# Hybrid conformer / RG-LRU decoder layer on eight cores: earlier first weights, a reordered gate schedule in two slots, and a last norm in place

## The chip, the cores and the metric

The kernel runs on all eight cores of one Trainium2 chip. Each core computes its own 1152 token rows (1024 of the prompt, 128 of the samples), and reads 1024 earlier prompt rows for the convolutions and the recurrent state. The cores exchange no data while they run. The metric is the device time of the slowest core, in microseconds (us).

Some executions of this program fall in a slower state, in which one die (cores 0 to 3, or 4 to 7) shows a lower granted TensorE clock. Times are set side by side only when they were taken on the same chip; across chips, ratios to the kernel before are compared.

Engine names are those of the profile: PE is TensorE, DVE is VectorE, ACT is ScalarE, POOL is GpSimd, SP is SyncE. POOL and SP mainly issue DMA transfers here.

## The reference

One layer: a mixer with two head groups on one shared input projection, then a gated MLP with a short convolution. Both are wrapped in RMS norms.

```python
def mixer(xn, ...):
    a_val, a_gate, b_x, b_gate = split(xn @ w_in)
    u  = a_val * sigmoid(a_gate)                     # group A, 8 x 128 channels
    ca = silu(layer_norm(causal_dwconv(u, 31 taps)))
    xc = causal_dwconv(b_x, 4 taps)                  # group B, 8 heads x 128 channels
    h  = rglru(xc, wa, wx, ...)                      # two gates per head, then a scan over tokens
    cb = h * gelu(b_gate)
    return concat(ca, cb) @ w_out

def layer(x):
    x = x + rms_norm(mixer(rms_norm(x, g_mix_pre)), g_mix_post)
    f = (gelu(g) * v) @ w_down       # g, v = halves of causal_dwconv(rms_norm(x) @ w_up, 3 taps)
    return x + rms_norm(f, g_ffn_post)
```

The width is 2048, the MLP's inner width 6144. Inputs and outputs are float32; matmul operands are bf16.

## The kernel before

The kernel is a list of operations with keys for what they read and write. A small scheduler derives the waits from the keys, and each engine runs its operations in the order written. Three places matter.

**The start.** Token tiles x0, x1, ... (128 rows of 2048 floats, 1 MB each) come on the SP queue. ACT and DVE norm a tile, PE transposes it, and ACT and DVE copy it out of PSUM (`p0_turn`). The first projection ("groups" g0 to g4 of columns) needs the transposed tiles and four weight tiles `wu0` to `wu3` (1 MB read, 512 KB stored each), which come on the POOL queue.

```python
p0_load(0)
load("sp", r_su, vecs[:, 0:V_FW], ...)
load_w(4, after=[("xt0",)])          # the four weight loads wait until x0 has landed
for n in range(1, 5):
    p0_load(n)
# ...
def next_tile(n):
    p0_turn(n)        # transpose tile n and copy it out of PSUM
    p0_norm(n + 2)    # norm tile n+2; this also issues a later reload of its buffer
next_tile(0)
next_tile(1)
for g in range(5):
    early(g, lambda j: next_tile(2 * g + 2 + j))     # projection of group g
    if g < 2:
        conv_diag(g)                                 # one DVE multiply of 4.28 us
```

**The slots.** In slots j = 3 to 7 PE alternates between the projections of group A and the two gates of a group B head. ACT and DVE work on what PE has left in PSUM.

```python
if j in (3, 4):
    P_gate(j - 3 + (j == 4), "wab"); P_sig(...)   # first gate: head 0 in slot 3, head 2 in slot 4
    if j == 3:
        P_conv(1)
# ... (v projection, head 0's or 2's second gate and scan)
if j == 3:
    P_gate(1, "wab"); P_sig(1, "p1", V_BA)
    bc = conv(j, [0])
    P_gate(1, "wxb"); P_sig(1, "p3", V_BX)
    conv_out(j, bc)
    P_in(1); P_mult(1)
    P_bx(2); P_evac(2)
    P_scan(1)
    P_conv(2)
```

**The tail.** The down-projection runs twice over halves of the inner width. The first half leaves partial sums in device memory (`f_scr`). The second half adds them, norms, adds the residual h (from `h_scr`) and stores y. There are nine token tiles t and four column groups fg.

```python
def hh_load(t):       # residual h of tile t, 1 MB, into one of three buffers, SP queue
    load("sp", r_x, T[f"hh{t % 3}"][:], h_scr[...], ..., [(f"hh{t % 3}", 0), (f"hh{t % 3}", 1)])
def down_load(i):     # 256 KB of partial sums into one of three prv buffers, SP queue
    load("sp", r_ld, T["prv"][:, i % 3, :], f_scr[rows, 512 * fg:512 * fg + 512], ...)
# ... for each item (fg, t):
    tt(f, out, T["prv"][:, i % 3, :], ALU.add, ...)            # "the add": frees the PSUM bank
    act(T["dj"][:], f, AF.Square, ..., accum=sc[:, fg:fg + 1])
    tt(f, f, T["grow3"][:, cs], ALU.mult, ...)
    # ... for fg == 3: sum, Ln, Exp, then
    stt(hh[:, 0:1536], f3, r, hh[:, 0:1536], ALU.mult, ALU.add, ...)
    stt(hh[:, 1536:2048], f, r, hh[:, 1536:2048], ALU.mult, ALU.add, ...)
    load("sp", r_out, y_d[rows, 0:1536], hh[:, 0:1536], ...)   # y stores, out of hh
    load("sp", r_out, y_d[rows, 1536:2048], hh[:, 1536:2048], ...)
    if t < 6:
        hh_load(t + 3)                                         # must wait for those stores
```

All buffers lie at fixed addresses in a table `AT`.

## Time and profile before

| What | Before |
|---|---|
| time, median of 3 runs | 1873.48 us (1871.01 to 1875.07) |
| spans of the eight cores in the profile | 1861.7 to 1869.5 us |
| PE busy, slowest core | 94% of the span |
| g0 / g2 start (median of cores) | 24.9 / 54.9 us |
| slot 2's convolution starts (mean of cores) | 136.7 us |
| from there to slot 4's convolution (mean) | 102.7 us |
| last matmul ends (mean) | 1833.2 us |
| tail: last matmul to the end (mean) | 32.5 us |

The last five rows are read from each core's timeline. They cut the kernel into four stages.

From the page of the profile (slowest core, core 4): busy time, share and number of instructions of each engine, then the shares of the chain of work that ended last.

```profile
PE 1751.6 (94%) x10302; PEld 916.9 (49%) x10470; DVE 988.8 (53%) x997; ACT 569.0 (30%) x1016; POOL 128.5 (7%) x239
PE 84%; DMA 7%; DVE 3%; ACT 3%; issue 2%; SPq 0%; POOL 0%; DVEq 0%; ACTq 0%; POOLq 0%
```

PE is the limit almost everywhere. What the change can win are the stretches in which PE waits, and the tail after its last matmul.

Start, timeline of PE before, core 4 (start, duration, engine, line, operation, output<-inputs, and in brackets the idle time before it and what ended it):

```profile
24.78 1.23 PE L379 MATMUL ps<-sb_xna_137,sb_wu_192 128*128 128x160 bf16 x8 [3.87 <-DVE sb_xna_137 L352]
...
29.51 1.47 PE L474 MATMUL ps<-sb_identb,sb_xs_107 128*128 128x128 bf16 x16
...
56.58 1.87 PE L379 MATMUL ps<-sb_xna_137,sb_wu_192 128*128 128x256 bf16 x8 [1.33 <-DVE sb_xna_137 L352]
```

These are the start of g0, the transposes of tile x2, and the start of g2. Both groups wait for a DVE copy of a transposed tile (`sb_xna`).

Start, timelines of ACT, then of DVE, before, core 4:

```profile
13.19 1.91 ACT L348 ACTIVATE sb_xs_102<-sb_xt_101 128x2048 bf16<-128x2048 f32 x1 [1.38 <-DMA sb_xt_101<-xall]
...
18.99 1.91 ACT L348 ACTIVATE sb_xs_107<-sb_xt_106 128x2048 bf16<-128x2048 f32 x1 [1.71 <-DMA sb_xt_106<-xall]
```

```profile
21.68 2.35 DVE L373 SCALAR_TENSOR_TENSOR sb_xs_107<-sb_xt_106,sb_tiny,sb_grow_51 128x2048 bf16<-128x2048 f32 x1 [2.78 <-ACT sb_tiny L346]
23.95 0.68 DVE L352 COPY sb_xna_137<-ps 128x1024 bf16<-128x1024 bf16 x1
```

ACT begins x1 at 13.19 and x2 at 18.99, each the moment the tile lands. The DVE lines show an order: the copy of tile x1 out of PSUM, which g0 needs, stands behind the norm of tile x2. So g0 waits for x2 to land although it does not use it.

Start, chain of work that ended last, before (start, duration, what):

```profile
10.84 24.98 DMA sb_wu_195<-w_in
36.57 10.33 DMA sb_xt_101<-xall
```

The last of the four weights takes from 10.84 to 35.82; only then is x0's buffer reloaded, because the weight load was given x0's buffer as a thing it reads.

Slots, waits of PE between 180 and 260 us, before, core 4 (waiting instruction, what ended the wait: us in all, times, longest):

```profile
PE ps L379 <- DVE sb_xcpbY L352: 4.2, 1, 4.2
PE ps L379 <- ACT sb_p3Y L346: 2.7, 2, 1.3
PE ps L379 <- ACT sb_p_68 L346: 1.3, 1, 1.3
...
```

Tail, chain before, core 4:

```profile
1836.56 9.18 DMA y<-sb_hh_108
...
1846.33 7.27 DMA sb_prv<-f_scr
...
1854.04 0.70 DVE sb_fl L364
```

A y store holds its `hh` buffer; the reload of that buffer waits for it on the SP queue; the load of the next partial sums stands behind that reload. The last matmul ended at 1834.6 on this core, but the last add could only start at 1854.04, when its partial sums had landed.

The last stores, timeline of the SP queue before, core 4 (span 1869.5):

```profile
1859.06 0.99 SPq L382 DMA_DIRECT2D y<-sb_hh_108  x2
```

The issue of the last two stores ends at 1860.05. The program ends 9.5 us later.

### The profile page before, as it was taken

To read this page: it belongs to the slowest core of one execution; us is meant where nothing else is said; L and a number is where in the kernel's file an instruction comes from. 1 tells how busy PE (TensorE), PEld (TensorE's weight loads), DVE (VectorE), ACT (ScalarE), POOL (GpSimd) and SP (SyncE) were. 2 spreads that over 40 slices of the span, in tenths; PEclk is the share of its full clock that TensorE was granted. 3 is DMA by queue.
4 is the path that set the end of the run, shared out by engine and by line. 5 is a ranking of instruction groups with operands and counts; after the bars stand their busy time and mean duration, and the time that the engine had idled before them with its cause. 6 is when DMAs were issued, how large, how long until landed. Compare 5 with 4: busy or idle time off the path is not lost.

```text
span 1869.5 us, 33611 instructions; the slowest of 8 cores (1861.7 to 1869.5 us)
## 1 busy us (share of the span) xinstructions
PE 1751.6 (94%) x10302; PEld 916.9 (49%) x10470; DVE 988.8 (53%) x997; ACT 569.0 (30%) x1016; POOL 128.5 (7%) x239
## 2 busy tenths in 40 slices
PE   6899899989987999999999999999999999999992
PEld 4675455644432444555555544444555555544441
DVE  3654455458875565666666630003666666652244
ACT  4552442368882443222222211111222222211111
POOL 0010000001120001000000000001000000000000
PEclk9899999999997999999999999999999999999996
DMA  8572243223278439543444326557343344455766
GB/s 218 175 160 41 41 83 53 37 35 58 36 123 214 158 143 195 103 68 68 68 68 68 68 61 119 119 118 128 67 69 67 67 70 68 69 137 119 186 187 201
DMA packets 54262, 193.22 MB, mean 103 GB/s; under 512 B 7233, under 2 KB 11201, under 8 KB 46785
## 3 DMA queue, kind: packets, MB, share of 16 engines
q0 software_dynamic: 29232, 106.41, 34.6%
q1 hardware_dynamic: 24850, 84.65, 13.7%
q8 instruction: 84, 1.38, 0.3%
q14 instruction: 96, 0.79, 0.1%
HBM read 266.52 MB, written 32.35 MB: 160 GB/s over the span
## 4 chain that ended last, share of the span: by engine, by line
PE 84%; DMA 7%; DVE 3%; ACT 3%; issue 2%; SPq 0%; POOL 0%; DVEq 0%; ACTq 0%; POOLq 0%
PE ps L379 83%; DMA sb_wo_213<-w_out 1%; DMA sb_wu_195<-w_in 1%; DMA sb_prv<-f_scr 1%; DMA y<-sb_hh_108 1%; PE ps L474 1%; DMA sb_xt_101<-xall 1%; ACT L346 1%; DMA y<-sb_hh_104 0%; PE ps L1139 0%; DMA sb_xt_96<-xall 0%; DVE sb_fl L364 0%; DMA y<-sb_hh_99 0%; DVE sb_ht L373 0%; DVE sb_xc_126 L373 0%
## 5 line engine op out<-in xcount | busy, mean ns | idle before, releaser
L352 DVE COPY sb_ve_120<-ps 128x1026 f32<-128x1026 f32 (+1 forms) x48 | 36.4, 801 | 297.8 <-PE ps L379 297.8
L352 DVE COPY sb_ve_134<-ps 128x1026 f32<-128x1026 f32 (+1 forms) x48 | 36.4, 800 | 113.9 <-PE ps L379 113.9
L373 DVE SCALAR_TENSOR_TENSOR sb_ov_136<-sb_ve_134,sb_vecs,sb_ov_136 128x1184 f32<-128x1184 f32 x48 | 69.7, 1451 | 5.3 <-DVE sb_ov_136 L373 0.5
L373 DVE SCALAR_TENSOR_TENSOR sb_og_135<-sb_ge_133,sb_vecs,sb_og_135 128x1184 f32<-128x1184 f32 x48 | 69.7, 1451 | 5.0
L373 DVE SCALAR_TENSOR_TENSOR sb_ov_122<-sb_ve_120,sb_vecs,sb_ov_122 128x1184 f32<-128x1184 f32 x48 | 69.7, 1451 | 5.0
L373 DVE SCALAR_TENSOR_TENSOR sb_og_121<-sb_ge_119,sb_vecs,sb_og_121 128x1184 f32<-128x1184 f32 x48 | 69.7, 1451 | 5.0
L344 ACT COPY sb_dstg<-ps 128x512 f32<-128x512 f32 x36 | 20.9, 586 | 159.6 <-PE ps L379 159.6
L379 PE MATMUL ps<-sb_ubf_110,sb_diag_109 128*128 128x342 bf16 (+3 forms) x527 | 62.3, 279 | 0.7 <-ACT sb_ca_199 L346 0.7
L379 PE MATMUL ps<-sb_ubf_124,sb_diag_123 128*128 128x342 bf16 (+3 forms) x527 | 62.3, 279 | 0.0
L344 ACT COPY sb_ffo<-sb_ve_134 128x32 f32<-128x32 f32 x24 | 5.3, 220 | 183.1 <-DVE sb_ve_134 L352 183.1
L344 ACT COPY sb_ffo<-sb_ve_120 128x32 f32<-128x32 f32 x24 | 5.3, 219 | 175.4 <-DVE sb_ve_120 L352 175.4
L346 ACT ACT_TABLE_LOAD x38 | 48.8, 1283 | 26.4 <-PE ps L379 14.1
L346 ACT ACTIVATE sb_og_135<-sb_og_135 128x1184 f32<-128x1184 f32 x24 | 28.6, 1190 | 82.5 <-DVE sb_og_135 L373 82.5
L379 PEld LDWEIGHTS ps<-sb_ubf_110,sb_diag_109 128*128 128x128 bf16 x527 | 44.8, 97 | 17.5 <-issue 0.9
L379 PEld LDWEIGHTS ps<-sb_ubf_124,sb_diag_123 128*128 128x128 bf16 x527 | 45.0, 97 | 17.1
L346 ACT ACTIVATE sb_og_121<-sb_og_121 128x1184 f32<-128x1184 f32 x24 | 28.6, 1190 | 79.6 <-DVE sb_og_121 L373 79.6
L344 ACT COPY sb_ge_119<-ps 128x1026 f32<-128x1026 f32 (+1 forms) x48 | 31.3, 704 | 34.2 <-PE ps L379 34.2
L344 ACT COPY sb_ge_133<-ps 128x1026 f32<-128x1026 f32 (+1 forms) x48 | 31.4, 706 | 27.4 <-PE ps L379 27.4
L379 PE MATMUL ps<-sb_xna_137,sb_wu_192 128*128 128x512 bf16 (+2 forms) x157 | 31.1, 348 | 8.0 <-DVE sb_xna_137 L352 5.2
L379 PE MATMUL ps<-sb_xn_139,sb_wp_216 128*128 128x512 bf16 (+1 forms) x188 | 34.8, 324 | 0.7 <-ACT sb_ge_119 L344 0.6
L379 PE MATMUL ps<-sb_xn_139,sb_wp_225 128*128 128x512 bf16 (+1 forms) x188 | 34.9, 324 | 0.2
L379 PE MATMUL ps<-sb_xn_142,sb_wp_217 128*128 128x512 bf16 (+1 forms) x190 | 35.0, 324 | 0.1
(728 smaller groups left out, 4053.4 us busy)
## 6 DMA issues: line engine op xcount, KB each, us to landing
f_scr<-sb_dstg SPq DMA_DIRECT2D x36, 256.0 KB, 3.1
sb_prv<-f_scr SPq DMA_DIRECT2D x36, 256.0 KB, 6.4
sb_xt_96<-xall SPq DMA_DIRECT2D x5, 1024.0 KB, 7.3
sb_x_0_117<-xall SPq DMA_DIRECT2D x5, 1024.0 KB, 4.8
h_scr<-sb_x_0_117 SPq DMA_DIRECT2D x5, 1024.0 KB, 3.9
sb_xt_101<-xall SPq DMA_DIRECT2D x4, 1024.0 KB, 10.3
sb_xt_106<-xall SPq DMA_DIRECT2D x4, 1024.0 KB, 13.9
sb_wp_214<-w_up POOLq DMA_DIRECT2D x8, 512.0 KB, 6.0
```

What stands on the lines that cost most here:

```text
L344: S.op("act", lambda e: e.copy(out=out, in_=in_), reads, writes)
L346: S.op("act", lambda e: e.activation(out=out, in_=in_, func=func, scale=scale, bias=bias), reads, writes)
L352: S.op("dve", lambda e: e.tensor_copy(out, in_), reads, writes)
L373: S.op("dve", lambda e: e.scalar_tensor_tensor(out, a, s, b, op0, op1), reads, writes)
L379: S.op("pe", lambda e: e.matmul(out, lhsT, rhs, start=start, stop=stop, skip_group_check=skip), reads, writes)
L474: S.op("pe", lambda e, pb=pb, j=j, k=k: e.transpose(pb[:, 128 * j:128 * j + 128], xs[:, 128 * k:128 * k + 128], identb[:]), [ks, "identb"] ...
```

## The change

The intent is to close the three gaps. (1) The four first weight tiles are issued at once, tiles x2 to x4 each wait for one of them, and x0's buffer is no longer tied to the weights. (2) In slots 3 and 4 head 1's and head 2's gates get more projection work between them. (3) The partial sums are loaded straight into their final buffers, the norm is done in place, and the residuals of tiles 6 to 8 go early into buffers that are free by then. The address table changes as a whole.

```diff
 # (1) start
-        load_w(4, after=[("xt0",)])
-        for n in range(1, 5):
-            p0_load(n)
+        load_w(4)
+        p0_load(1)
+        for n in range(2, 5):
+            p0_load(n, [(f"wu{n - 1}",)])
...
             if g == 2:
-                load_w(6, after=[("xt3",)])
+                load_w(6, after=[("xt4",)])
 # (2) slots
-            if j in (3, 4):
-                P_gate(j - 3 + (j == 4), "wab")
-                P_sig(j - 3 + (j == 4), "p1", V_BA)
-                if j == 3:
-                    P_conv(1)
-            else:
+            if j == 3:
+                P_gate(0, "wab")
+                P_sig(0, "p1", V_BA)
+                P_conv(1)
+            elif j > 4:
...
-            proj(bv, "v", j, ACT3)
+            proj(bv, "v", j, ACT3, only=0)
+            proj(bv, "v", j, ACT3, only=1)
+            if j == 4:
+                P_gate(2, "wab")
+                P_sig(2, "p1", V_BA)
+            proj(bv, "v", j, ACT3, only=2)
...
             if j == 3:
+                bc = conv(j, [0])
                 P_gate(1, "wab")
                 P_sig(1, "p1", V_BA)
-                bc = conv(j, [0])
+                conv_out(j, bc)
+                bx2 = triple()
+                P_bx(2, bx2)
                 P_gate(1, "wxb")
...                                   # head 2's P_conv now ahead of head 1's P_scan
 # (3) tail
-            ("fl", [2, 512], F_, 22.9, 24),
-            ("prv", [3, 512], F_, 22.9, 24), ("dstg", [3, 512], F_, 21, 22),
+            ("fl", [3, 512], F_, 22.9, 24), ("fh", [3, 512], F_, 22.9, 24),
+            ("dstg", [3, 512], F_, 21, 22),
...
+            def f_load(t, fg):      # partial sums straight into f3 (SP queue), fg 3 into the fl ring (POOL queue)
+                f, kf = f_place(t, fg)
+                load("sp" if fg < 3 else "pool", ..., f, f_scr[...], [("f_scr", t, fg)], [kf])
+            def f_place(t, fg):
+                if fg < 3:
+                    return T[f"f3{t}"][:, fg, :], (f"f3{t}", fg)
+                return T["fl"][:, t % 3, :], ("fl", t % 3)
+            def h_place(t): ...     # tiles 0-5: hh ring; tiles 6-8: f30..f32 and fh (POOL queue)
...
-                tt(f, out, T["prv"][:, i % 3, :], ALU.add, PK(b) + [("prv", i % 3)], [kf])
+                tt(f, out, f, ALU.add, PK(b) + [kf], [kf])
...
+                for c0, c1 in ((0, 768), (768, 1536)) if tt_ == 8 else ((0, 1536),):
+                    kk = k3[c0 // 512:(c1 + 511) // 512]
+                    stt(f3[:, c0:c1], f3[:, c0:c1], r, ha[:, c0:c1], ALU.mult, ALU.add, kk + [kr] + kha, kk)
+                    load("sp", r_out, y_d[rows, c0:c1], f3[:, c0:c1], kk, [])
+                stt(f, f, r, hb, ALU.mult, ALU.add, [kf, kr, khb], [kf])
+                if tt_ < 3:
+                    hh_load(tt_ + 3)
+                load("sp", r_out, y_d[rows, 1536:2048], f, [kf], [])
                 if tt_ < 6:
-                    hh_load(tt_ + 3)
+                    f_load(tt_ + 3, 3)      # into the buffer that the store above has just been given
+                if tt_ < 3:
+                    hh_load(tt_ + 6)
```

## The prediction

> **What bounds it now.** TensorE: the page gives PE 94% busy of 1869.5 us; the chain of waits is 84% PE. The stage table (windows) shows 99% or more for most of 800 to 1830 us. Only idle PE can give time (core 4):
> - Start: PE busy 35 of the first 60 us. Chain: "DMA sb_wu_195", 25 us. The four weight loads waited on tile xt0 and so count as its readers; the slot's reload is issued only at 36.0 us, when the last weight lands (35.8). Group g2 starts at 56.6 us.
> - Slots 3 and 4 (180 to 240 us): PE waits 1.3 (p3Y), 1.3 (p), 4.2 (xcpbY), 0.2 and 1.3 us (p3Y), 8.4 together; matmuls after the 4.2 us gap run slow (2.45 for 1.67, 0.98 for 0.58 us), another 1.2.
> - Tail: last matmul ends at 1834.5, span at 1869.5: 35 us (31 to 35 over the cores). Chain: y store, h reload, prv load, in order on the SP queue: each prv load sits behind an h reload that waits 5 to 9 us for its buffer's y store.
>
> **What the change does.**
> 1. Start. Weights go out at 2 us with x0 and x1; x2 to x4 wait for weights 1 to 3; the reload of x0's slot no longer waits for weight 3. At the 3.5 us per MB read that the first 36 us show (9.4 MB in 34 us), weight 3 lands near 27 us, tile 5 near 37 (43 before). But x2 lands near 24 instead of 19, and VectorE, in order, evacuates tile 1 only after normalising tile 2: g0 starts at 29 to 31 instead of 24.8. g2 starts near 52. Gain 4.5 us (0 to 8).
> 2. Slots. Head 1's two gates get 6.7 us of projection between them; head 2's conv goes ahead of head 1's scan and its gate 15 us later, inside the v projection. One wait of about 0.4 us stays. Gain 9 us.
> 3. Tail. Partial sums are preloaded into f3 in place (no prv), results written in place, h of tiles 6 to 8 fetched early into freed f3 buffers. Behind a y store sit only fl loads: tiles 7 and 8 wait for the fl stores of 4 and 5 (stores take 5 to 9 us, loads 6). I estimate the last add 3 to 4 us after the last matmul (20 before), then 4 us to the first half store and 9 us for the last megabyte (10 before). The Trainium skill ("DMA: Bandwidth & Descriptors", Anatomy of one DMA) puts about 2 us fixed on each DMA; here a 256 KB store takes 3.1 us, which agrees, so splitting helps little. Tail 16.5 instead of 35 us: gain 18 (14 to 22).
>
> Moved buffers change nothing I can find.
>
> **Sum.** 4.5 + 9 + 18 = 31.5, perhaps 2 more for less spread between cores: about 1840 us, 8 in 10 between 1830 and 1852. Faster by over 2% needs 1836.7: chance 0.32; within 2% 0.67; slower 0.01.
>
> **Right if** g2 starts 2 to 7 us earlier; no PE wait over 1 us between 180 and 240 us; the span ends 14 to 20 us after the last matmul. **Wrong if** weights starve x1 (g0 after 33 us); ScalarE's table switches delay head 2 and its gate still waits; the fl ring delays the last add beyond 8 us; or PE loses time later.

## More of the kernel before

**The end of the program.** The SP engine waits for every DMA that was ever issued.

```python
fin = Op("sp", None, False)
fin.deps = [o for n in self.NAMES for o in self.streams[n] if o.is_dma]
```

## The result

The changed kernel took 1862.74 us, the median of 4 runs (1861.02 to 1864.39). The kernel before took 1873.48 us beside it on the same chip (median of three runs; a fourth, slow one took 2124.55). The ratio is 0.9944, with a 95% interval of 0.9925 to 0.9964: about 10.5 us faster, which is "within 2%". Executions over 1.5% slower than the fastest of the same kernel are left out of the means. All ratios here are the mean time of one kernel's runs over that of the other's of the same rounds, so they are not quite the ratio of the quoted medians. The result lies 10.7 us above the predicted range of 1830 to 1852 us.

Stage by stage, mean over the eight cores in the two profiled executions:

| Stage | Before | After | Gain | Predicted gain |
|---|---|---|---|---|
| start, up to slot 2's convolution | 136.7 | 143.1 | -6.4 | +4.5 |
| slot 2's to slot 4's convolution | 102.7 | 93.6 | +9.1 | +9 |
| from there to the last matmul | 1593.9 | 1594.0 | -0.1 | 0 |
| tail | 32.5 | 26.6 | +5.9 | +18 |
| mean span | 1865.7 | 1857.2 | +8.5 | |

The four gains add up to the change of the mean span. One stage came out as predicted, one gained a third of what was expected, and one lost. Of the 31.5 us predicted, 23 are missing: 10.9 at the start and 12.1 in the tail.

The page after (slowest core, core 1), the same two lines:

```profile
PE 1761.6 (95%) x10470; PEld 916.4 (49%) x10470; DVE 989.3 (53%) x998; ACT 569.3 (31%) x1016; POOL 134.5 (7%) x254
PE 89%; DMA 4%; ACT 2%; DVE 2%; issue 2%; POOL 0%; DVEq 0%; ACTq 0%; POOLq 0%; SPq 0%
```

PE's busy time seems to have grown by 10 us. It has not: the trace before lacks 168 matmul records (10302 against 10470).

Start, timeline of PE after, core 1:

```profile
25.08 1.86 PE L474 MATMUL ps<-sb_identb,sb_xs_102 128*128 128x128 bf16 x16 [9.68 <-DVE sb_xna_137 L352]
34.75 1.23 PE L379 MATMUL ps<-sb_xna_137,sb_wu_192 128*128 128x160 bf16 x8 [7.81 <-DVE sb_xna_137 L352]
...
38.71 1.06 PE L474 MATMUL ps<-sb_identb,sb_xs_107 128*128 128x128 bf16 x16
...
61.45 1.07 PE L379 MATMUL ps<-sb_xna_137,sb_wu_192 128*128 128x256 bf16 x8 [3.16 <-DVE sb_xna_137 L352]
```

The first line is the transposes of x1. g0 starts 10.0 us later than on core 4 before, the transposes of x2 9.2 us later, g2 4.9 us later. (As medians over the cores these are 10.5, 10.3 and 7.2 us; core 4 before had the latest g2 of all.) Once g0 runs it no longer waits for a weight, but it runs late.

Start, timelines of ACT, then of DVE, after, core 1:

```profile
19.23 1.91 ACT L348 ACTIVATE sb_xs_102<-sb_xt_101 128x2048 bf16<-128x2048 f32 x1 [9.20 <-DMA sb_xt_101<-xall]
...
28.96 1.91 ACT L348 ACTIVATE sb_xs_107<-sb_xt_106 128x2048 bf16<-128x2048 f32 x1 [6.18 <-DMA sb_xt_106<-xall]
```

```profile
31.66 2.35 DVE L373 SCALAR_TENSOR_TENSOR sb_xs_107<-sb_xt_106,sb_tiny,sb_grow_51 128x2048 bf16<-128x2048 f32 x1 [6.72 <-ACT sb_tiny L346]
33.92 0.68 DVE L352 COPY sb_xna_137<-ps 128x1024 bf16<-128x1024 bf16 x1
```

This is the cause at the start. x1 lands at 19.2 instead of 13.2, x2 at 29.0 instead of 19.0. The copy that g0 waits for is still the next DVE instruction after the norm of x2.

Where the bandwidth went is in the list of DMA issues after, core 1, 0 to 40 us (transfer, queue, KB, us from issue to landing):

```profile
sb_wu_192<-w_in POOLq DMA_DIRECT2D x1, 512.0 KB, 9.9
sb_wu_193<-w_in POOLq DMA_DIRECT2D x1, 512.0 KB, 16.2
```

The first two weights were issued at 2.2 and 2.8 us, so they landed at about 12 and 19 us, before g0 could use them. x1 was issued at 2.8 us and landed at 19.1 (13.1 before). The Trainium skill ("DMA: Bandwidth & Descriptors", Queues, rings and completion order) says that each DMA engine takes turns between the queue rows it has work for, a packet at a time. This trace agrees, counted in the packets that the profile lists. DMA queues after, core 1, first from 9 to 12 us, then from 12 to 16 us (q0 carries the weights, q1 the tokens; number of packets, MB written, share of the 16 DMA engines):

```profile
q0 software_dynamic: 109, 0.38, 87.5%
q1 hardware_dynamic: 114, 0.09, 16.0%
```

```profile
q1 hardware_dynamic: 79, 0.64, 51.6%
q0 software_dynamic: 79, 0.32, 50.7%
```

From 12 to 16 us x1's packets (8 KB each) and the weights' (4 KB written, from 8 KB of floats) alternate one for one, so x1 gets half of the DMA time. From 9 to 12 us the token queue got as many turns as the weights, but almost no bytes: 88 of its 114 packets are the 32-byte packets of `flags`, a small table of 4 KB that stands ahead of x1 on the SP queue. On this core `flags` landed at 12.6 us, against 9.9 on core 4 before; over all cores it was 12.5 to 14.4 against 8.6 to 10.9. So part of x1's delay was spent on 4 KB of small packets, each of which waited for its turn beside a 4 KB packet of weights. No run moves `flags` behind x1, so what that would gain is not shown.

Slots, waits of PE between 180 and 260 us, after, core 1:

```profile
PE ps L379 <- DVE sb_ubf_124 L364: 1.2, 1, 1.2
PE ps L379 <- ACT sb_p1Y L346: 0.2, 1, 0.2
```

8.4 us of waits have become 1.4. (The lines of other engines are left out here and above. The prediction had allowed no wait over 1 us in slots 3 and 4; one of 1.2 us is there.) The 4.2 us wait before had a second cost: the matmuls after it took 2.45 us for groups that take 1.67 elsewhere. The Trainium skill ("TensorE: Matmul & The Clock Gate", Part 1) has TensorE fall to half its clock after an idle window of about 3.4 us. This trace agrees: the granted clock was 0.50 from 222.1 to 223.2 us, just after the 4.2 us wait (before, core 4), and in the timeline of PE above, the 16 transposes after a 9.68 us wait took 1.86 us, those without a wait 1.06. The start is not so sharp: before, on core 4, the transposes of x1 took 1.87 us after a wait of only 2.93.

Tail, chain after, core 1:

```profile
1805.82 16.11 DMA y<-sb_fl
...
1825.00 7.24 DMA sb_fl<-f_scr
1832.33 0.70 DVE sb_fl L364
...
1847.93 2.39 DMA y<-sb_f_191
```

The old chain of `hh` and `prv` is gone. A shorter one of the same kind took its place: a 256 KB store of y out of an `fl` buffer took 16.11 us, and the load of tile 6's partial sums into the same buffer had to wait for it. (The store landed at 1821.9 and the load was issued at 1825.0. This further 3.1 us is there on every core, where the other loads of the ring mostly follow within 0.6 us; the trace does not show what it is.) The add of tile 6 starts at 1832.33, after the last matmul (1831.0). Tiles 7 and 8 follow at the pace of DVE and ACT, 5.5 to 5.8 us each.

Tail, timeline of DVE after, core 1: the add of tile 6, the add of tile 8, and the second half of tile 8's result.

```profile
1832.33 0.69 DVE L364 TENSOR_TENSOR sb_fl<-ps,sb_fl 128x512 f32<-128x512 f32 x1 [7.81 <-DMA sb_fl<-f_scr]
...
1843.66 0.68 DVE L364 TENSOR_TENSOR sb_fl<-ps,sb_fl 128x512 f32<-128x512 f32 x1
...
1850.41 1.02 DVE L373 SCALAR_TENSOR_TENSOR sb_f_191<-sb_f_191,sb_ssf,sb_f_185 128x768 f32<-128x768 f32 x1 [2.61 <-DMA y<-sb_f_191]
```

The last line is a wait that the change made itself. Keys are kept per 512 columns. The halves (0, 768) and (768, 1536) both hold the key of columns 512 to 1023, so the second half waits for the first half's store to land.

The last store, timeline of the SP queue after, core 1 (span 1862.8):

```profile
1852.22 0.33 SPq L382 DMA_DIRECT2D y<-sb_fl  x1
```

This store has 256 KB, and the one just ahead of it 384 KB, against 1 MB before. Yet the program ends 10.3 us after this issue. That raises the question whether the 9.5 us before were the time of the last megabyte at all. One difference between the compiled programs points elsewhere: SP's final list has 178 wait instructions before and 194 after. And the traces record when a store lands: on core 4 before, the last one landed 3.5 us after the start of its issue, 6.3 us before the end; on core 1 after, 2.7 us after, 7.9 us before the end.

### The profile page after: what moved, and what is told of

The parts are those of the page before. It is cut to its first block, busy times and chain, and to the rows that moved or that the text cites. A ratio compares the mean times of both kernels' runs of the same rounds, so it can differ in the third digit from the quotient of the medians.

```text
span 1862.8 us, 33795 instructions; the slowest of 8 cores (1849.1 to 1862.8 us)
## 1 busy us (share of the span) xinstructions
PE 1761.6 (95%) x10470; PEld 916.4 (49%) x10470; DVE 989.3 (53%) x998; ACT 569.3 (31%) x1016; POOL 134.5 (7%) x254
## 4 chain that ended last, share of the span: by engine, by line
PE 89%; DMA 4%; ACT 2%; DVE 2%; issue 2%; POOL 0%; DVEq 0%; ACTq 0%; POOLq 0%; SPq 0%
PE ps L379 88%; DMA sb_wo_213<-w_out 1%; DMA sb_wu_194<-w_in 1%; DMA y<-sb_fl 1%; PE ps L474 1%; DMA sb_xt_98<-xall 1%; PE ps L1146 0%; DMA sb_fl<-f_scr 0%; ACT L346 0%; DVE sb_fl L364 0%; DVE sb_ht L373 0%; ACT sb_xs_1_132 L348 0%; ACT sb_t_1_128 L346 0%; ACT sb_dj L348 0%; DVE sb_t_1_129 L729 0%
## 5 line engine op out<-in xcount | busy, mean ns | idle before, releaser
L346 ACT ACT_TABLE_LOAD x38 | 48.8, 1283 | 28.8 <-PE ps L379 16.5
L379 PE MATMUL ps<-sb_xna_137,sb_wu_192 128*128 128x512 bf16 (+2 forms) x160 | 29.7, 333 | 17.1 <-DVE sb_xna_137 L352 14.9
L344 ACT COPY sb_ge_133<-ps 128x1026 f32<-128x1026 f32 (+1 forms) x48 | 31.4, 707 | 27.4 <-PE ps L379 27.4
L379 PE MATMUL ps<-sb_xn_139,sb_wp_214 128*128 128x512 bf16 (+1 forms) x192 | 35.2, 325 | 0.5 <-DVE sb_xn_139 L352 0.5
```

Of the source, the lines that this page charges most:

```text
L344: S.op("act", lambda e: e.copy(out=out, in_=in_), reads, writes)
L346: S.op("act", lambda e: e.activation(out=out, in_=in_, func=func, scale=scale, bias=bias), reads, writes)
L379: S.op("pe", lambda e: e.matmul(out, lhsT, rhs, start=start, stop=stop, skip_group_check=skip), reads, writes)
```

## The experiments

All fourteen kernels gave correct results. Each was timed in five rounds beside the kernel before on its own chip. "Worth" figures are differences of ratios, times 1872 us. With the intervals of the table such a figure is uncertain by about 3 us either way, and with the first run's 0.9944 as the base instead of 0.9954 all would shift by 1.9 us; the stage times are the firmer evidence. The mean start of slot 2's convolution ("start stage") and the tail are read as in the tables above.

The main theory was this: at the start the weights take the bandwidth that x1 and x2 need; the slots work as planned; and the tail loses its gain to the `fl` ring and to something fixed at the end. The rivals: the new address table costs time everywhere; the start's loss comes from the added waits on x2 to x4; the end is really the time of the last stores.

| Kernel | Time (us), median | Ratio to before | 95% interval |
|---|---|---|---|
| a: start undone | 1856.57 | 0.9911 | 0.9898 to 0.9924 |
| b: tail undone | 1870.15 | 0.9986 | 0.9973 to 1.0000 |
| c: slots undone | 1874.27 | 1.0006 | 0.9994 to 1.0018 |
| d: no waits on x2 to x4 | 1859.88 | 0.9929 | 0.9917 to 0.9941 |
| the change, again | 1863.54 | 0.9954 | 0.9942 to 0.9967 |
| e: fl ring in weight buffers | 1865.06 | 0.9978 | 0.9948 to 1.0009 |
| f: fewer last waits | 1854.04 | 0.9905 | 0.9891 to 0.9918 |
| g: copies first | 1858.59 | 0.9947 | 0.9917 to 0.9977 |
| h: a, f and a new tail | 1847.43 (1837.93 undisturbed) | 0.9868 | 0.9824 to 0.9913 |
| i: h, weights after `vecs`, no mark on x0 | 1842.60 | 0.9844 | 0.9828 to 0.9860 |
| j: i, waits and copies first | 1841.96 | 0.9840 | 0.9826 to 0.9854 |
| k: j without waits on x2 to x4 | 1842.64 | 0.9842 | 0.9828 to 0.9856 |
| l: h, diagonals earlier | 1849.58 (slower chip) | 0.9850 | 0.9832 to 0.9868 |
| m: l and copies first | 1849.23 (slower chip) | 0.9849 | 0.9832 to 0.9867 |

a to d ran on one chip (before: 1872.39 us), the change again and e to g on a second (1871.87), h to k on a third (1872.09), l and m on a fourth (1878.04).

### The change again

No edit: the changed kernel on another chip.

> The changed kernel as it is, for the same rounds as the next three. Every theory: about 1862 us, ratio to the kernel before 0.994.

It came to 0.9954, against 0.9944 the first time. Its start stage ends at 142.9 us on average and its tail is 26.7 us. So the stage table is not an accident of one execution, and 0.9954 is the base for the differences below.

### a: the start undone

```diff
-        load_w(4)
-        p0_load(1)
-        for n in range(2, 5):
-            p0_load(n, [(f"wu{n - 1}",)])
+        load_w(4, after=[("xt0",)])
+        for n in range(1, 5):
+            p0_load(n)
```

> The changed kernel with the load order of the start put back as it was before (weights after the first token tile, token tiles 2 to 4 without waits, the reload of the first slot again behind the weights). Theory 1 (the weights take bandwidth from token tiles 1 and 2, and VectorE in order holds tile 1's evacuation behind tile 2's norm): group g2 starts at about 55 us again instead of 61.5, the whole kernel takes 6 to 8 us less than the changed one, about 1855 us. Rival (the later start is of no account, since later stages wait for other things; the lost time is all in the tail): about 1862 us.

This is faster than the change, by 0.0043 or 8 us. The start stage ends at 136.5 us, as before the change (136.7), with the new address table in place. That shows that the loss of 6 to 7 us at the start comes from the order of the loads, and that the moved buffers cost nothing there.

### b: the tail undone

```diff
-            dn = {} ... f_load / f_place / h_place, norm in place, fl ring of 3, fh
+            dn = {"n": 0} ... down_load / prv / hh ring, as before
```

> The changed kernel with the tail of before (partial sums through three rotating buffers, results in the residual buffers), all else as changed. The changed kernel's tail from the last matmul is 23 to 32 us over the cores, before it was 31 to 35. Theory (the new tail is worth only about 6 us on the slowest cores): 1868 to 1872 us, tail again 31 to 35 us. Rival (the new tail is worth its predicted 18 us and something else lost time): about 1880 us.

The tail is back to 30.5 to 33.7 us and the kernel is 0.0032 (6 us) slower than the change. The new tail is worth 6 us, which agrees with the 5.9 us of the stage table.

### c: the slots undone

```diff
-            if j == 3: P_gate(0, "wab") ... P_conv(2) ahead of P_scan(1)
+            if j in (3, 4): P_gate(j - 3 + (j == 4), "wab") ... as before
```

> The changed kernel with slots 3 and 4 in the order of before. Theory (slots gained 8.5 us, as the start of the conv of slot 4 against that of slot 2 shows: 93.6 us after, 102.1 before): 8 to 9 us more than the changed kernel, about 1871 us. Rival (the slots' gain is given back later, in the stage from 400 to 600 us that ScalarE and VectorE limit): the same as the changed kernel.

This is 0.0052 (9.7 us) slower than the change. The stretch from slot 2's to slot 4's convolution takes 103.0 us on average, where the change takes 93.6. The slots give what was predicted. One thing is left over: the last add comes only 2.3 to 5.8 us after the last matmul here, against 3.9 to 12.6 in the change with the same tail code. The traces show where: the store of tile 3, which the ring passes on, took 6.0 to 8.3 us here and 8.3 to 16.1 in the change. No run says why it was quicker here.

### d: no waits on x2 to x4

```diff
-            p0_load(n, [(f"wu{n - 1}",)])
+            p0_load(n)
```

> The changed kernel with the weights still first, but token tiles 2 to 4 no longer waiting for weights. If the weights ahead of the tiles cost the time, g0 still starts near 34 us and the time stays near 1862. If the waits of tiles 2 to 4 cost it (tile 2 is issued only at 19 us), g0 starts at 28 us or earlier and the time falls by about 5 us.

The start stage ends at 138.7 us and the kernel is 4.7 us faster than the change. g0 starts at 31.6 us (35.4 in the change, 24.9 before). So the added waits are more than half of the loss, but not all of it: without them, early weights still hold x1 back (its transposes start at 25.6 us, against 18.9 before).

### g: copies out of PSUM ahead of the norms

```diff
-        next_tile(0)
-        next_tile(1)
+        p0_turn(0)
+        p0_turn(1)
+        p0_norm(2)
+        p0_norm(3)
```

> The changed kernel, with the transposes of tiles 0 and 1 both ahead of the norms of tiles 2 and 3, so that VectorE and ScalarE evacuate tile 1 without waiting for tile 2. Theory (the in-order engines hold tile 1 behind tile 2, which lands near 29 us): g0 starts at 27 to 29 us instead of 35, g1 somewhat earlier, g2 by 2 to 6 us. Rival (tile 1's own late landing at 19 us sets everything): g0 moves by less than 2 us.

Beside the change again, on the same chip, g0 starts at 28.1 us instead of 35.5, as the DVE order said it should. g2 starts at 57.3 instead of 61.7, and the start stage ends at 139.0 instead of 142.9. In time the gain is unclear (0.9947 against 0.9954; one of its runs took 1872.8 us and widens the interval). Freeing the copy moves g0 by 7 us but what follows by about 4; g2 also needs tiles that come later.

### e: tiles 4 to 8 of the fl ring moved into weight buffers

```diff
             def f_place(t, fg):
+                if t > 3:
+                    return T[f"wp{t - 4}"][:].bitcast(F32)[:, 0:512], (f"wp{t - 4}",)
...
+                if g == 1 and (fg, tt_) == (2, 8):     # the last weight tile of fg 2 is used up
+                    for t in range(4, 9):
+                        f_load(t, 3)
...
-                if tt_ < 6:
-                    f_load(tt_ + 3, 3)
+                if tt_ == 0:
+                    f_load(3, 3)
```

> The changed kernel, with the last quarter's partial sums of tiles 4 to 8 loaded into weight buffers that are dead after the third quarter, so that no load waits for a store of y; tile 3 keeps the small ring. Theory (the ring of three holds the last adds: on the slowest core the load for tile 6 waits 16 us for the store of tile 3): the last add of all cores comes 3 to 8 us after the last matmul, where the changed kernel has 2 to 13 us, the tail is 22 to 26 us on every core instead of 23 to 32, the time falls by 4 to 6 us. Rival (the DMA engines are full, so the loads come late in any case): less than 2 us.

This missed. It takes the wait for the stores away, but the loads can only go out once the weight buffers are free, and then they queue with three h loads on POOL. Timeline of DVE, e, core 3:

```profile
1822.19 0.69 DVE L364 TENSOR_TENSOR sb_wp<-ps,sb_wp 128x512 f32<-128x512 f32 x1 [11.86 <-DMA sb_wp<-f_scr]
```

The first of these adds waits 11.86 us, then the others follow at DVE's pace, and the last add is 6.7 to 10.9 us after the last matmul: no better than the change. (The profiled execution was the one of 1882.7 us, with cores 4 and 5 at a lower clock, which also widens the interval; core 3 is undisturbed.) A buffer that is free of one wait but loaded later gains nothing; the loads have to be issued earlier.

### f: fewer waits at the end of the program

```diff
-        fin.deps = [o for n in self.NAMES for o in self.streams[n] if o.is_dma]
+        last = {}
+        for n in self.NAMES:
+            for o in self.streams[n]:
+                if o.is_dma and (o.sem.num not in last or last[o.sem.num].val < o.val):
+                    last[o.sem.num] = o
+        fin.deps = list(last.values())
```

One wait for each semaphore's last DMA implies all the earlier ones; 41 wait instructions are left.

> The changed kernel, with the end of the program waiting for each of the 51 DMA semaphores once, at its last value, instead of for every DMA in turn: 41 wait instructions on the SP queue instead of 194. Theory (these waits stand behind the last store on that queue and take 0.045 us each, as the trace's waits and the gaps between them do, 8.7 us in all, while the last store lands in about 3): the time falls by 5 to 7 us. Rival (the end waits for the last store to land): no change.

This is 0.0049 (9 us) faster than the change. The last store, timeline of the SP queue, f, core 4 (span 1852.6):

```profile
1849.59 0.33 SPq L387 DMA_DIRECT2D y<-sb_fl  x1
```

The end is 2.7 us after the issue of the same 256 KB store, not 10.3. About 7.5 us of what looked like the last store was SP working through its list. The wait instructions on SP after the last store, before (core 4), after (core 1) and f (core 4) (count, ns of one, start of the first and of the last):

```profile
L178 SPq EVENT_SEMAPHORE  x178: 17/17/17, 1860.1 to 1869.3; - x178
```

```profile
L178 SPq EVENT_SEMAPHORE  x194: 17/17/17, 1852.6 to 1862.6; - x194
```

```profile
L183 SPq EVENT_SEMAPHORE  x41: 17/17/17, 1850.0 to 1852.3; - x41
```

Before and after, one wait follows the other about every 0.05 us, long after the last store has landed, and the time from that store's issue to the end is the same on all eight cores (9.5 and 10.3 us), however long the store took. In f it is not: there the last wait is passed when the store lands, and the end comes 0.3 us after the landing on every core. So f has reached the time of the store itself (2.0 to 3.0 us from issue to landing). The tail as a whole is 8.5 us shorter than in the change again (18.2 against 26.7 on average); the 1 us beyond the list is that the last adds came a little sooner, which f did not aim at.

### h: the start of before, fewer last waits, and a tail without the ring

```diff
                 # start as in a, last waits as in f
             def f_place(t, fg):
-                return T["fl"][:, t % 3, :], ("fl", t % 3)
+                if t < 6:
+                    nm = ("fl", "fh")[t // 3]
+                    return T[nm][:, t % 3, :], (nm, t % 3)
+                return T[f"wp{t - 6}"][:].bitcast(F32)[:, 0:512], (f"wp{t - 6}",)
...
                 if g == 1 and (fg, tt_) == (1, 8):
-                    for t in range(3):
+                    for t in range(6):
                         f_load(t, 3)
...
-                for c0, c1 in ((0, 768), (768, 1536)) if tt_ == 8 else ((0, 1536),):
+                for c0, c1 in ((0, 1024), (1024, 1536)) if tt_ == 8 else ((0, 1536),):
...
-                if tt_ < 6:
-                    f_load(tt_ + 3, 3)
```

Partial sums of tiles 0 to 5 get a buffer each and are loaded early; those of 6 to 8, and a quarter of their residuals, go into freed weight buffers. No load waits for a y store.

> The slots of the change; the start of before; each semaphore waited for once at the end; and a new tail: the last quarter's partial sums of tiles 0 to 5 have a buffer each from the start (the small ring and the buffer that held the last quarters of the residuals), those of tiles 6 to 8 and the last quarters of their residuals go into dead weight buffers, and tile 8's store is split on a buffer boundary (1024) so that the second half's arithmetic waits for no store. Theory: g2 at 54 to 56 us; last add 2 to 4 us after the last matmul on every core; 6 us from it to the last store's issue instead of 9; 2 to 3 us to the end: a tail of 11 to 13 us, in all about 1840 us. Rival (the DMA engines are full, late loads hold the last adds wherever they are put): last add 6 to 10 us after the last matmul, about 1845 us.

Two executions took 1837.93 and 1838.95 us. Two others took 1855.9 and 1856.1, with cores 6 and 7 about 15 us longer than the rest at a granted clock of 0.971; they pull the median and the ratio up. The profiled execution was one of these. In its six undisturbed cores (0 to 5) the last matmul ends at 1824.1 us on average, as in a.

Tail, timeline of DVE, then of the SP queue, h, core 1 (span 1837.9):

```profile
1832.27 1.95 DVE L378 SCALAR_TENSOR_TENSOR sb_f<-sb_f,sb_ssf,sb_f 128x1024 f32<-128x1024 f32 x2 [0.76 <-ACT sb_ssf L351]
```

```profile
1835.01 0.33 SPq L387 DMA_DIRECT2D y<-sb_wp  x1
```

The two parts of tile 8's result (x2, split at 1024 on a key's border) now run back to back, where the change waited 2.61 us. On every core the last add is 1.5 or 1.6 us after the last matmul, the last store is issued 6.2 us after that, and the end follows 2.5 to 3.8 us later. The tail is 10.3 to 11.5 us, against 22.3 to 27.4 in a. The tail of before (32.5 us) is shorter here by 22 us, more than the 18 predicted. 15.4 of them are the earlier last add and 6.7 the end after the last store's issue (9.5 before, 2.8 here), where the list was shortened. h changes the ring, the split and the list together; only the list has a run of its own (f), so the other shares are read from the timelines.

### i: weights after `vecs`, without the mark on x0's buffer

The chain of waits before had blamed the mark that ties x0's reload to the weights. i removes that tie from h: the weights now wait for a small early load (`vecs`) instead of for x0.

```diff
-        load_w(4, after=[("xt0",)])
+        load_w(4, after=["vecs"])
```

> As h_all_tail, with the four weights waiting for the vector constants, which land at about the same time as token tile 0, instead of for tile 0 itself: the same start as before, but without the read mark that held the reload of tile 0's slot until the last weight had landed. Theory of the prediction (that mark delayed tile 5 and with it g2): g2 starts 3 to 6 us earlier than in h_all_tail. Rival (with the reload early, tile 5 takes bandwidth from the weights, g0 and g1 start later): no gain.

This missed. x1 is not held back (the transposes of x2 start at 30.2 us, against 29.2 before), but g2 starts at 59.0 us, 4 us later than before, and the start stage ends at 141.1 instead of 136.5. Timelines of PE at the start: first h, core 0, then i, core 0: the third and fourth weights' matmuls of g0.

```profile
31.59 2.29 PE L384 MATMUL ps<-sb_xna,sb_wu 128*128 128x160 bf16 x16 [2.20 <-DMA sb_wu<-w_in]
35.04 2.29 PE L384 MATMUL ps<-sb_xna,sb_wu 128*128 128x160 bf16 x16 [1.16 <-DMA sb_wu<-w_in]
```

```profile
35.57 2.29 PE L384 MATMUL ps<-sb_xna,sb_wu 128*128 128x160 bf16 x16 [3.96 <-DMA sb_wu<-w_in]
41.23 2.29 PE L384 MATMUL ps<-sb_xna,sb_wu 128*128 128x160 bf16 x16 [3.37 <-DMA sb_wu<-w_in]
```

With the tie gone, tile x5's reload goes out at 13.7 us instead of 35.2 and lands at 35.8 instead of 41.2 (means over the cores, h beside i). But the weights arrive later: the first by 1.1 us, the second by 1.3, the third by 2.5 and the fourth by 5.7 (40.7 against 35.0). They were issued 1.6 us later, because `vecs` lands after x0; the rest of the fourth's delay falls where x5's load runs beside it. The tie had been keeping x5 out of the way of the weights. The late reload in the chain before was a true link of the chain, but removing it made the stage longer. No run removes the tie and leaves the weights' issue where it was.

### j and k: copies first, with and without waits on the tiles

```diff
 # j, against i (k has the second part only)
-        for n in range(1, 5):
-            p0_load(n)
+        p0_load(1)
+        for n in range(2, 5):
+            p0_load(n, [(f"wu{n - 2}",)])
...
-        next_tile(0)
-        next_tile(1)
+        p0_turn(0)
+        p0_turn(1)
+        conv_diag(0)
+        p0_norm(2)
+        p0_norm(3)
...
-            if g < 2:
-                conv_diag(g)
+            if g == 1:
+                conv_diag(1)
```

> As i_gated_weights, with token tiles 2, 3 and 4 waiting for weights 0, 1 and 2, tiles 0 and 1 transposed and evacuated ahead of the norms of 2 and 3, and the first diagonal built ahead of them too. Theory: g0 at 22 to 24 us, weights all in by 31 us, g2 at 47 to 50 us, 5 to 7 us less than h_all_tail. Rival (bandwidth alone sets g2): g2 as in i_gated_weights.

> As j_gated_evac, but tiles 2 to 4 without waits. If the order on VectorE matters and the waits don't, g2 as in j_gated_evac; if the waits matter, the weights land at 36 us, g0's second half waits for them, and g2 lies between i_gated_weights and j_gated_evac.

In j g0 starts at 20.5 us, the earliest of all so far, yet g2 starts at 57.4 and the start stage ends at 138.4. In k it is 21.9, 57.5 and 138.7. An early g0 does not carry over, and j's expectation (g2 at 47 to 50) missed. The two come to the same g2 by different ways: in j x2 landed late (28.7 us, 19.2 in h) and the fourth weight early (30.9), in k x2 early (17.5) and the fourth weight late (40.7). Both kernels are steady (1842.0 and 1842.6 us) because of the tail they have from h.

### l and m: the diagonals moved out of the way

What g2 waits for is DVE. The 4.28 us multiply `conv_diag(0)` stands between g0 and the copies that g2 needs. l moves it into the time in which DVE waits for tiles; m also does the copies first.

```diff
 # l, against h (m: p0_turn(0), p0_turn(1), conv_diag(0), p0_norm(2), p0_norm(3))
         next_tile(0)
-        next_tile(1)
+        p0_turn(1)
+        conv_diag(0)
+        p0_norm(3)
         for g in range(5):
             early(g, lambda j: next_tile(2 * g + 2 + j))
-            if g < 2:
-                conv_diag(g)
+            if g == 1:
+                conv_diag(1)
```

> As h_all_tail, with the first 4.3 us diagonal on VectorE moved from between g0 and g1 to the gap before the norm of token tile 3. Over ten kernels g2 starts 22.6 to 25.5 us after the transposes of tile 2, unless the weights of g0 are late. Theory (that stretch is VectorE's in-order work, the diagonal among it: it stands ahead of the evacuation of tile 4): g2 starts 2 to 4 us earlier than in h_all_tail, 20 to 22 us after tile 2, the time falls by as much, to about 1836 us. Rival (the arrival of tile 5, which is reloaded at 36 us and lands at 43, sets the end of the stretch): no change.

> As l_diag_early, with tiles 0 and 1 transposed ahead of the norms of tiles 2 and 3 too, and the diagonal ahead of both norms. If only tile 2's arrival and the work after it count, the same as l_diag_early, though g0 starts at 22 us instead of 24.7. If g0's start counts (as the prediction took it), g2 comes another 2 us earlier.

Timelines of DVE at the start: h, core 0, then l, core 1: the multiply and the copy that follows g0.

```profile
45.30 4.28 DVE L369 TENSOR_TENSOR sb_diag<-sb_identb,sb_vecs 128x3968 bf16<-128x3968 bf16 x1
49.50 0.68 DVE L357 COPY sb_xna<-ps 128x1024 bf16<-128x1024 bf16 x1
```

```profile
24.24 4.28 DVE L369 TENSOR_TENSOR sb_diag<-sb_identb,sb_vecs 128x3968 bf16<-128x3968 bf16 x1
...
45.10 0.68 DVE L357 COPY sb_xna<-ps 128x1024 bf16<-128x1024 bf16 x1
```

In l g2 starts at 52.2 us (54.7 in h) and the start stage ends at 134.0 (136.5 in h, 136.7 before). That is 2.5 us, the first gain at the start against before. It rests on one execution of each kernel; the cores of one execution differ by 4 to 5 us, but a, h and before agree within 0.2 us on the mean, and m, with the same multiply moved, has 134.6. In m g0 starts at 21.1 us and g2 at 52.7: again the early g0 brings nothing, which was a miss. On their chip die 0 had a lower clock (0.975), so their times cannot be set beside those of h to k. So a gain in time is not shown. On die 1 the cores of l end at 1828.0 to 1836.6 us.

No kernel here is over 2% faster than before. All of h to m beat both kernels; the lowest ratio is j's, 0.9840, and the lowest time 1837.93 us, in an undisturbed execution of h.

## Why the prediction was right or wrong

**What bounds the kernel: right.** PE is over 99% busy in most of the middle (800 to 1830 us; 84% from 400 to 600, before, core 4), and the middle did not change (1593.9 and 1594.0 us).

**Slots, "Gain 9 us": right.** 9.1 us by stage, 9.7 us by undoing it (c). The waits fell from 8.4 to 1.4 us. One wait of 1.2 us is left where 0.4 was expected.

**Start, "Gain 4.5 us (0 to 8)": wrong in sign.** The stage lost 6.4 us, and undoing it gained 8 us (a). Two steps failed.
- "x2 lands near 24 instead of 19 ... g0 starts at 29 to 31". x2 landed at 29.0 and g0 started at 35.4. I used one rate for all transfers together and overlooked that x1 would share it from 2 us on, turn by turn, and that the small packets of `flags` stand ahead of it. x1 landed 6 us late, and x2 was then also made to wait for the second weight (at 19 us). The prediction named this case ("weights starve x1, g0 after 33 us"), but only among the ways in which it could be wrong. d shows that the waits on the tiles are the larger part of the loss (4.2 us of the start stage, 4.7 us in time).
- "g2 starts near 52". The chain of waits blamed the late reload, and so the mark on x0's buffer. i removed the mark with x1 undisturbed; x5 landed 5.4 us earlier, and still g2 came 4 us later, because the weights came late. So the early reload bought nothing. What the runs show the stage to follow is the order of DVE's work (l: moving 4.28 us of it gained 2.5 us) and the sharing of bandwidth between tiles and weights.

**Tail, "Tail 16.5 instead of 35 us: gain 18": the mechanism was right, two terms were mis-sized.**
- "the last add 3 to 4 us after the last matmul". It was 3.9 to 12.6 us, 7.3 on average. I put the stores at 5 to 9 us from the trace of before. In the full stretch of the change one 256 KB store took 16.11 us, and the ring passed that on. DVE's and ACT's 5.5 us or more for each tile do not allow the chain to catch up. h, without the ring, has 1.5 us. The prediction had named "the fl ring delays the last add beyond 8 us" as a danger; that happened on four of the eight cores.
- "then 4 us to the first half store and 9 us for the last megabyte (10 before)". The first half store was issued 4.3 us after the last add (1843.66 to 1847.93), as predicted. From there to the end it took 14.9 us, not 9: 2.61 us are the wait that the split at 768 made, and 10.3 us come after the last store's issue. Of those, f took 7.5 us away by shortening the list of waits, so the "9 us for the last megabyte" was mostly no transfer at all: before, the last store landed 3.0 to 4.1 us after its issue, and the other 5.4 to 6.5 us were SP's waits. I had named a stretch of the trace without looking for what was in it.

**"2 more for less spread between cores": wrong.** The spans spread by 7.8 us before and by 13.7 after. The ring hits the cores differently (tails of 31.0 to 35.0 us before, 23.0 to 31.8 after), and the ends of the last matmul spread more too (by 6.8 us before, 9.3 after), for which no cause is shown.

**"Moved buffers change nothing": held.** With the start undone the start stage is as before (a), and with the tail undone so is the tail (b).

What stays open: why the store of tile 3, and with it the last add, is quicker in one kernel than in another with the same tail code (last add 3.7 us after the last matmul on average in c, 7.3 in the change); how much of x1's delay `flags` makes; and what puts two cores of h at a lower clock in some executions.

## What to carry to other kernels

Sending data earlier only helps if nothing that is needed sooner shares the bandwidth: before moving a load, ask which transfer it will run beside, and which instruction, in the order of its engine, waits for that one. A buffer ring that is refilled behind a store inherits the store's worst time, not its median; give the last tiles their own buffers, loaded before the stores begin. And look at the end of a program by itself: whatever lies between the last store's issue and the end may be the program's own list of waits.

## What the Trainium skill lacked or had wrong

- "DMA: Bandwidth & Descriptors", Anatomy of one DMA: it gives about 2.0 us fixed and the rest by bytes for one DMA, and names the DMA path of GpSimd. For 256 KB that is 2.6 us, as an estimate by its formula. The 36 stores of 256 KB of partial sums here, issued by SP, took 3.1 us (before) and 2.7 us (after) in the median, which is near. With the DMA engines full (busy share 0.95 from 1800 to 1830 us), such a store took 16.11 us. The section says nothing on how far such a time can stretch, and that is what set the tail.
- The same page, Queues, rings and completion order: the turns by packets were as it says (79 and 79 packets from 12 to 16 us). It does not spell out what they do to a load of small packets: `flags`, 4 KB in packets of 32 bytes, landed at 12.6 us beside the weights and at 9.9 us without them.
- I found no page on the cost of a long list of semaphore waits at the end of a program. Here it was 7.5 us: the time from the last store's issue to the end was 10.3 us with 194 waits on SP, 2.7 us with 41.
